# A batched x·yᵀ on one core: four half-stored rows remade in sixteen pieces, one for each DMA engine, and stored through GpSimd's queue

## The chip, the cores and the metric

The kernel runs on one core of a Trainium2 chip. The metric is device time in microseconds (us), lower is better. Before the change three runs took 297.93, 297.98 and 298.37 us, with a median of 297.98.

## The reference

```python
batch, n_heads, seq_t, seq_s, channels = 8, 12, 512, 512, 64
x: (8, 12, 512, 64) float32      y: (8, 12, 512, 64) float32
out = einsum('bhtc,bhsc->bhts', x, y)      # (8, 12, 512, 512) float32
```

For each of 96 (batch, head) pairs a 512 x 512 product of x with y transposed over 64 channels. 25.17 MB are read and 100.66 MB are written.

## The kernel before, in words

**Tiles.** The 96 heads are taken in 6 groups of 16, each group in two halves of 8 heads. A half makes 4 output tiles, so there are 48, numbered o = 0 to 47. A tile has 128 partitions of 4096 float32 (16 KB each, 2 MB in all) and covers two heads: partition p = 2q + u holds 8 full output rows (8 x 512) of head u, block q. Even partitions belong to one head, odd partitions to the other, and each partition is one contiguous 16 KB run in DRAM.

**Stages.** Loads of x and y (2 MB each, `load`, L177, on SyncE's queue, SP) are cast to bf16 and rearranged by ScalarE (ACT), VectorE (DVE) and GpSimd (POOL) in `compress` and `mix`, then transposed in 32 x 32 blocks by DVE (`transposes`, L225 and L234). TensorE (PE) makes a tile in two groups of four 128x512 matmuls (`products`, L248), one group into each of two PSUM buffers `pm0` and `pm1`. ACT copies PSUM into the output buffer (`copy`, L140); only the last tile, o = 47, is copied by DVE (L142). There are three pairs of output buffers (`pair`), each of two tiles.

**Stores.** All output goes through SP's hardware queue (queue 1 in the profile), but for a small share described below. Tiles 0 to 7 are stored one by one (2 MB). From tile 8 on, two tiles of one pair are stored together (4 MB, `transfer`, L161). The last four tiles are an exception: tile 44 (`SHARED`) is stored by `shares`, tile 45 alone (2 MB, L331), tiles 46 and 47 together (4 MB).

**What `shares` does.** Tile 44 is cut so that the core's 16 DMA engines get different amounts. The even partitions go in one transfer on SP's queue, 4 partitions to an engine. The odd partitions are taken in two halves b = 0 and b = 1. Of each half POOL's software queue (queue 0) takes three transfers, of 5, 3 and 8 engines with two partitions each: the first five engines get only columns 0 to 1023 of each partition (4096 B), the other eleven get the whole 16 KB. For the first four engines, SP's queue carries the remaining 3072 columns (`HELD` = 6 x 512; 12288 B). What is left are the 3072 **held columns** of the fifth engine's two partitions in each half: four rows of 12 KB, 48 KB, that this engine never carries.

**What `rest` does.** At the very end PE computes the held columns again (`again`, L298) into `pm0`: four pieces of 768 columns for each half, written in 20 small matmuls so that the pieces of one half lie in partitions 0 to 15. One DVE copy (L142, 16 x 1536) puts them into `xk0`, an input buffer that is no longer in use. Two SP transfers of 24 KB store them, each over four engines, two runs of 3072 B an engine and transfer. They are the last two transfers on SP's queue, behind the 4 MB store of tiles 46 and 47.

**Order and end.** The program order is written out by hand. `emit` waits for what an instruction needs, emits it and records it; `need` leaves out waits that are known to have been met. Each buffer's DMAs count on a semaphore of their own (`dma0`, `dma2`, ... for SP, `dmapool` for POOL). At the end POOL waits for all semaphores but two and clears them in three instructions (L412), then waits for `dmapool` and clears it, then for `dma2` (`LAST`, that of the 4 MB store and of the held pieces) and clears it (L415). That is the program's last instruction.

Of the kernel before, what the change touches and what calls it, by code (L numbers as in the profile page):

```python
# [9 lines left out]
def kernel(  # L10
# [3 lines left out]
    y: bass.AP,  # L14
    out: bass.AP,
):

# [4 lines left out]
    nc = tc.nc  # L24
    B, H, T, C = x.shape
    _, _, S, _ = y.shape
    P = 128
# [5 lines left out]
    V = G // 4  # L33
    K = 8
# [3 lines left out]
    N = K * S  # L38
    SINGLE = 2 * V
    SHARED = V * NH - V  # L40
    LAST = (V * NH - SINGLE - 2) // 2 % 3 * 2
    HELD = 6 * S
    fp32 = mybir.dt.float32
    bf16 = mybir.dt.bfloat16
    u32 = mybir.dt.uint32
# [9 lines left out]
    def buffer(name, width, dtype):  # L55
        return nc.alloc_sbuf_tensor(name, [P, width], dtype)[:, :]
# [4 lines left out]
    xks = [  # L61
        extra[:, :N // 2].bitcast(bf16) if i == 1 else buffer(f"xk{i}", R * C, bf16)
        for i in range(NG - 1)
    ]
# [9 lines left out]
    xTs = [buffer(f"xT{i}", K * D * E, u32) for i in range(2)]  # L74
    yTs = [buffer(f"yT{i}", D * R // 2, u32) for i in range(2)]
    pms = [nc.alloc_psum_tensor(f"pm{i}", [P, 4, S], fp32)[:, :, :] for i in range(2)]
    engines = {"act": nc.scalar, "dve": nc.vector, "pool": nc.gpsimd, "pe": nc.tensor, "sp": nc.sync}
    sems, ticks, snaps, writer, readers = {}, {}, {}, {}, {}
    known, own = {e: {} for e in engines}, {e: {} for e in engines}

    def need(name, points, told=True):

        best = {}
        for p, v in points:
            if known[name].get(p, 0) < v:
                best[p] = max(best.get(p, 0), v)
        for p, v in list(best.items()):
            if any(snaps[q, w].get(p, 0) >= v for q, w in best.items() if q != p):
                del best[p]
        for p, v in best.items():  # L90
            if told:
                engines[name].wait_ge(sems[p], v)  # L92
            known[name][p] = v
            for q, w in snaps[p, v].items():
                known[name][q] = max(known[name].get(q, 0), w)

    def promise(name, reads, writes):

        points = [writer[r] for r in (*reads, *writes) if r in writer]
        points += [v for w in writes for v in readers.get(w, ())]  # L100
        if name == "pool" and name in ticks:
            points.append((name, ticks[name]))
        return points

    def record(name, p, step, reads, writes, queue=False):
        at = (p, ticks.get(p, 0) + step)
        ticks[p] = at[1]
        if not queue:
            own[name][p] = at[1]
        snaps[at] = {**known[name], **own[name], p: at[1]}  # L110
        for r in reads:
            readers.setdefault(r, []).append(at)
        for w in writes:
            writer[w], readers[w] = at, []

    def signal(p):
        if p not in sems:
            sems[p] = nc.alloc_semaphore(p)
        return sems[p]

    def emit(name, make, reads=(), writes=(), dma=None, by=None, step=1):
        need(name, promise(name, reads, writes))
        p = by or name
        if dma is not None:
            p, step = f"dma{dma}", 16
        make().then_inc(signal(p), step)
        record(name, p, step, reads, writes, dma is not None)

    loaded = {}

    places = [0, 1, 2, 3, 4, 0, 1, 2, 3, 4, 1, 3]
    alone = [0, 2, 4, 0, 1, 3, 2, 4]
    heads = [0, 2, 1, 3]
# [3 lines left out]
    def copy(name, dst, src, reads, writes, by=None):  # L137
        emit(
            name,
            lambda: nc.scalar.activation(dst, src, COPY)  # L140
            if name == "act"
            else engines[name].tensor_copy(dst, src),  # L142
            reads,
            writes,
            by=by,
        )

    def both(*ids):
        return [("slot", i, pm) for i in ids for pm in range(2)]

    def place(ap, pattern):
        name = ap.tensor.name
        return mybir.PhysicalAccessPattern(
            ap=pattern, offset=ap.offset, dtype=ap.dtype, memref=name, memsetref=f"{name}_set"
        )

    def transfer(name, dst, src, to=None, of=None):

        to = to or dst.ap
        of = of or [src.ap[0], *[[1, 1]] * (len(to) - len(src.ap)), *src.ap[1:]]  # L160
        return engines[name].add_instruction(  # L161
            mybir.InstDMACopy(
                name=nc.get_next_instruction_name(),
                engine=engines[name].engine,
                ins=[place(src, of)],
                outs=[place(dst, to)],
                mode="Copy",
                cce_op=mybir.AluOpType.bypass,
                queue={"sp": "qSPDynamicHW", "pool": "qPoolDynamic"}[name],
            )  # L170
        )
# [82 lines left out]
    def all_products():  # L254
# [3 lines left out]
        with nc.Fori(1, V * NH + 1, 2 * V, engines=[nc.tensor.engine]) as first:  # L258
            for half in range(2):
                for j, h in enumerate(heads):  # L260
# [3 lines left out]
                    for p in range(2):  # L264
                        nc.tensor.wait_ge(sems[f"free{p}"], first + at)
                        products(half, h, 4 * p).then_inc(signal("pe"), 1)

    def shares(o, s):

        to, mine = ov[o // V, heads[o % V]], slots[s]  # L270
        line, w = to.ap[0][0], N - HELD

        def part(name, p, n, k, lo=0, hi=N):

            dst, src = to[p // 2:p // 2 + n, p % 2, lo:hi], mine[p:p + 2 * n - 1:2, lo:hi]
            emit(
                name, lambda: transfer(name, dst, src, [[line * n // k, k], [line, n // k], [1, hi - lo]]),
                reads=both(s), dma="pool" if name == "pool" else s,
            )

        for b in range(2):
            for p, n, k, hi in ((1, 10, 5, w), (21, 6, 3, N), (65, 16, 8, N)):
                part("pool", 32 * b + p, n, k, 0, hi)
        emit("sp", lambda: transfer("sp", to[:, 0], mine[::2]), reads=both(s), dma=s)
        for b in range(2):
            part("sp", 32 * b + 1, 8, 4, w)

    def again():

        half, h, part = SHARED // V % 2, heads[SHARED % V], HELD // 4  # L290
        xT = xTs[half].bitcast(bf16).rearrange("p (k h m) -> p k h m", k=K, h=V)
        yT = yTs[half].bitcast(bf16)
        for c in range(3, -1, -1):
            begin, end = N - HELD + c * part, N - HELD + (c + 1) * part
            cuts = sorted({begin, end, *range(begin, end, S), *(n for n in range(0, N, S) if begin < n < end)})
            for lo, hi in zip(cuts, cuts[1:]):
                for b in range(2):
                    last = nc.tensor.matmul(  # L298
                        pms[0][:4 * c + 4, 2 * b + (lo - begin) // S, (lo - begin) % S:(lo - begin) % S + hi - lo],
                        xT[:, lo // S, h, 32 * b + 16 - 4 * c:32 * b + 20],  # L300
                        yT[:, h * S + lo % S:h * S + lo % S + hi - lo], start=True, stop=True,
                    )
        return last

    def rest():

        half, part = SHARED // V % 2, HELD // 4
        to = ov[SHARED // V, heads[SHARED % V]]
        mine = xks[0][:16].bitcast(fp32)[:, :2 * part].rearrange("p (b s) -> p b s", b=2)
        emit("pe", again, [("xT", half), ("yT", half)], [("pm", 0)])  # L310
        copy(
            "dve", mine, pms[0][:16].rearrange("p (b j) s -> p b (j s)", b=2)[:, :, :part],
            [("pm", 0)], [("xk", 0)],
        )
        for b in range(2):
            dst, src = to[16 * b + 8:16 * b + 10, 1, N - HELD:], mine[1::2, b]
            emit(
                "sp", lambda: transfer(
                    "sp", dst, src, [[part, 4], dst.ap[0], [1, part]], [src.ap[0], [1, 1], src.ap[-1]]
                ),  # L320
                reads=[("xk", 0)], dma=LAST,
            )

    def store(o):
# [72 lines left out]
    for o in range(V, V * NH):  # L397
        result(o)
        if o % V == V - 1:
            prepare(o // V + 2)  # L400
    all_products()
    rest()
    emit("sp", nc.sync.nop)

    last = f"dma{LAST}"
    late = ["dmapool", last]
    others = [p for p in sems if p not in late]
    need("pool", [(p, ticks[p]) for p in others])
    numbers = sorted(sems[p].num for p in others)
    runs = [n for n in numbers if n - 1 not in numbers]  # L410
    for n in runs:
        nc.gpsimd.sem_clear(range(n, next(m for m in range(n, n + len(sems) + 1) if m not in numbers)))  # L412
    for p in late:
        need("pool", [(p, ticks[p])])
        nc.gpsimd.sem_clear(sems[p])  # L415


# [28 lines left out]
```

## Time and profile before

| | us |
|---|---|
| median of three runs | 297.98 |
| the profiled execution's own time | 297.92 |
| its span in the profile | 296.1 |
| outside the span | 1.8 |
| ACT busy | 208.2 |
| DVE busy | 158.0 |
| PE busy | 139.9 |
| POOL busy | 59.5 |
| written to and read from HBM | 125.8 MB, 425 GB/s over the span |

How to read it: the span runs from the first to the last instruction of the program. "Busy" leaves out waiting and the issuing of DMAs. The profile's page has a row of 40 digits for the DMA engines, the mean busy share of all 16 in tenths (9 is 90% or more), and the same row can be asked for over any stretch of time. A DMA is carried by several engines, each working through its own packets; the trace holds every packet with its queue, start, duration and size, though not with its engine. A transfer's packets end on each engine with one of 4 bytes, which counts up the semaphore.

### The profile page before, as it was taken

Reading aid. Unit: us, or ns where it says so; the run is one execution under the profiler, and the core shown is the slowest. Engines: PE = TensorE matmul, PEld = TensorE weight load, DVE = VectorE, ACT = ScalarE, POOL = GpSimd, SP = SyncE. Lnnn points to the kernel's source line nnn. Section 1 sums busy time; section 2 is a strip of 40 time slices with the busy share of each in tenths; the row PEclk is TensorE's granted clock in tenths of the full one; section 3 lists DMA queues with packets and bytes.
Section 4 is the critical chain, followed back from the end, with each engine's and each line's share of the span. In section 5 each row is a group of like instructions: output and inputs, shape, how many; then the busy total and the mean of one; then the engine's idle time right before and its main releaser. Section 6 shows DMA issues by size and latency. Waiting matters only on the chain.

```text
span 296.1 us, 1231 instructions
## 1 busy us (share of the span) xinstructions
PE 139.9 (47%) x404; PEld 37.9 (13%) x404; DVE 158.0 (53%) x76; ACT 208.2 (70%) x107; POOL 59.5 (20%) x29
## 2 busy tenths in 40 slices
PE   0000040437576557556654655577546646575400
PEld 0000010112111111111111111111111111121200
DVE  2167798899929594925808529258095240002600
ACT  1664666999999999666966696669666976684000
POOL 2399999992000000000000000000000000040000
PEclk9999995657779997778789776765798787756855
DMA  7999999999999999999999999999999999999998
GB/s 272 427 429 427 432 429 427 432 425 425 427 438 427 460 425 426 425 429 447 429 456 426 425 429 425 425 438 434 434 456 425 425 429 429 425 438 422 415 436 348
DMA packets 6178, 125.85 MB, mean 425 GB/s; under 512 B 896, under 2 KB 896, under 8 KB 932
## 3 DMA queue, kind: packets, MB, share of 16 engines
q1 hardware_dynamic: 5888, 125.03, 98.7%
q0 software_dynamic: 288, 0.80, 0.7%
q14 instruction: 2, 0.02, 0.0%
HBM read 25.17 MB, written 100.66 MB: 425 GB/s over the span
## 4 chain that ended last, share of the span: by engine, by line
DMA 56%; ACT 23%; PE 7%; issue 4%; DVE 3%; SPq 0%; ACTq 0%
DMA out_dram<-pair 43%; ACT pair L140 21%; DMA pair<-in_y_dram 7%; DMA pair<-in_x_dram 6%; PE pm L248 6%; DVE pair L142 3%; ACT xk L140 1%; PE pm L298 1%; ACT yb L140 1%; DVE xk L142 1%; SPq L177 0%; ACTq L92 0%; SPq L371 0%; SPq L367 0%
## 5 line engine op out<-in xcount | busy, mean ns | idle before, releaser
L248 PE MATMUL pm<-yT,xT 128*128 128x512 bf16 x384 | 136.6, 501 | 137.3 <-ACT pair L140 100.0
L140 ACT ACTIVATE pair<-pm 128x2048 f32<-128x2048 f32 x94 | 170.6, 1883 | 41.3 <-DMA out_dram<-pair 37.5
L225 DVE STREAM_TRANSPOSE xT<-xb 128x2048 uint32<-128x2048 uint32 x12 | 46.7, 3893 | 69.1 <-PE pm L248 66.7
L248 PEld LDWEIGHTS pm<-yT,xT 128*128 128x128 bf16 x384 | 36.0, 115 | 237.0 <-ACT pair L140 156.0
L161 POOL DMA_DIRECT2D out_dram<-pair x6 | 3.5, 583 | 193.7 <-ACT pair L140 193.7
L142 DVE COPY xb<-xk 32x2048 bf16<-32x2048 bf16 x32 | 41.7, 1304 | 0.9
L142 DVE CAST yb<-pair 64x2048 bf16<-64x2048 f32 x10 | 30.7, 3074 | 9.5 <-DMA pair<-in_y_dram 9.3
L140 ACT ACTIVATE xk<-pair 128x4096 bf16<-128x4096 f32 x5 | 18.1, 3617 | 10.4 <-DMA pair<-in_x_dram 10.3
L142 POOL COPY xb<-xk 32x2048 bf16<-32x2048 bf16 x8 | 23.5, 2939 | 6.7 <-ACT xk L140 6.2
L142 DVE COPY pair<-pm 128x2048 f32<-128x2048 f32 x2 | 4.5, 2286 | 31.9 <-PE pm L248 31.9
L234 DVE STREAM_TRANSPOSE yT<-yb 128x1024 uint32<-128x1024 uint32 x10 | 19.2, 1918 | 0.0
L140 ACT ACTIVATE yb<-pair 64x2048 bf16<-64x2048 f32 x5 | 12.4, 2472 | 3.9 <-DMA pair<-in_y_dram 3.8
L142 POOL CAST yb<-pair 64x2048 bf16<-64x2048 f32 x5 | 14.5, 2903 | 1.2 <-DMA pair<-in_y_dram 0.8
L142 POOL COPY xb<-pair 32x2048 bf16<-32x2048 bf16 x4 | 12.7, 3184 | 0.3
L140 ACT ACTIVATE pair<-pair 128x4096 bf16<-128x4096 f32 (+1 forms) x2 | 6.1, 3030 | 3.7 <-DMA pair<-in_x_dram 2.5
L142 DVE CAST pair<-pair 64x2048 bf16<-64x2048 f32 x2 | 5.4, 2694 | 4.0 <-DMA pair<-in_y_dram 4.0
L142 DVE COPY xb<-pair 32x2048 bf16<-32x2048 bf16 x4 | 5.2, 1306 | 0.1
L140 ACT ACT_TABLE_LOAD x1 | 1.3, 1283 | 4.4 <-PEq L371 4.4
L378 DVE MEMSET xb<- 128x2048 uint32 x1 | 1.8, 1765 | 4.9 <-PEq L371 4.9
L234 DVE STREAM_TRANSPOSE yT<-pair 128x1024 uint32<-128x1024 uint32 x2 | 3.9, 1946 | 0.0
L298 PE MATMUL pm<-yT,xT 128*16 128x256 bf16 (+5 forms) x20 | 3.3, 333 | 0.6 <-DVE pair L142 0.6
L142 POOL CAST pair<-pair 64x2048 bf16<-64x2048 f32 x1 | 3.3, 3293 | 0.1
(7 smaller groups left out, 5.8 us busy)
## 6 DMA issues: line engine op xcount, KB each, us to landing
out_dram<-pair SPq DMA_DIRECT2D x19, 4096.0 KB, 21.8
out_dram<-pair SPq DMA_DIRECT2D x9, 2048.0 KB, 9.3
pair<-in_x_dram SPq DMA_DIRECT2D x6, 2048.0 KB, 18.8
pair<-in_y_dram SPq DMA_DIRECT2D x6, 2048.0 KB, 16.5
out_dram<-pair SPq DMA_DIRECT2D x1, 1024.0 KB
out_dram<-pair POOLq DMA_DIRECT2D x2, 256.0 KB, 16.6
out_dram<-pair SPq DMA_DIRECT2D x2, 96.0 KB
out_dram<-pair POOLq DMA_DIRECT2D x2, 96.0 KB, 14.6
```

The source lines that it names most:

```text
L140: lambda: nc.scalar.activation(dst, src, COPY)
L142: else engines[name].tensor_copy(dst, src),
L161: return engines[name].add_instruction(mybir.InstDMACopy(name=nc.get_next_instruction_name(), engine=engines[name].engine, ins=[place(src, ...
L225: lambda: nc.vector.transpose(xTs[half].rearrange("p (k r e) -> p k e r", k=K, e=E), xbs[half].rearrange("p (k e c) -> p k e c", k=K, e=E),),
L234: lambda: nc.vector.transpose(yTs[half].rearrange("p (r j) -> p j r", r=D), ybs[half][b].rearrange("p (j c) -> p j c", c=D),),
L248: last = nc.tensor.matmul(pms[k // 4][:, j, :], xT[:, k + j, h, :], yT[:, h * S:(h + 1) * S], start=True, stop=True,)
L298: last = nc.tensor.matmul(pms[0][:4 * c + 4, 2 * b + (lo - begin) // S, (lo - begin) % S:(lo - begin) % S + hi - lo], xT[:, lo // S, h, 32 ...
L378: lambda: engines[name].memset(xbs[half], 0.0),
```

## The change

The held columns become 7 x 512 = 3584 for each of the four rows, 14 KB a row and 56 KB in all. So in `shares` the first five engines get 512 columns (2048 B) instead of 1024 of each partition through POOL's queue, and SP's two transfers for the first four engines grow to 14336 B a partition.

`again` now cuts the 3584 columns of each half into 8 pieces of 448 and makes them in 28 matmuls, so that piece q = 0 to 7 of half b lies in partitions 64b + 4q to 64b + 4q + 3, its two held rows in the second and fourth of them: partitions 0 to 31 and 64 to 95 in all. DVE's copy becomes 96 x 448. Instead of two SP transfers behind the 4 MB store, `rest` issues three transfers on POOL's queue, for 5, 3 and 8 engines, two runs of 448 columns (1792 B) an engine. At the end both late semaphores are waited for together and cleared in one instruction; the others too are cleared in one.

```diff
-    HELD = 6 * S
+    HELD = 7 * S
...
+    turns = [(0, 5), (5, 3), (8, 8)]
...
+    late = [f"dma{LAST}", "dmapool"]
+    for p in late:
+        signal(p)
...
+    def part(name, dst, src, k, reads, dma):
+        assert src.ap[0][1] == 2 * k and dst.ap[0][1] == k
+        emit(
+            name, lambda: transfer(name, dst, src, dst.ap),
+            reads=reads, dma=dma,
+        )
     def shares(o, s):
         to, mine = ov[o // V, heads[o % V]], slots[s]
-        line, w = to.ap[0][0], N - HELD
-        def part(name, p, n, k, lo=0, hi=N):
-            dst, src = to[p // 2:p // 2 + n, p % 2, lo:hi], mine[p:p + 2 * n - 1:2, lo:hi]
-            emit(
-                name, lambda: transfer(name, dst, src, [[line * n // k, k], [line, n // k], [1, hi - lo]]),
-                reads=both(s), dma="pool" if name == "pool" else s,
-            )
+        w = N - HELD
+        def odd(name, b, e, k, lo, hi):
+            p = 4 * e + 32 * b + (32 if e > 7 else 0)
+            n = 2 * k
+            dst = to[p // 2:p // 2 + n, 1, lo:hi].rearrange("(k i) n -> k i n", i=2)
+            part(name, dst, mine[p + 1:p + 2 * n:2, lo:hi], k, both(s), "pool" if name == "pool" else s)
         for b in range(2):
-            for p, n, k, hi in ((1, 10, 5, w), (21, 6, 3, N), (65, 16, 8, N)):
-                part("pool", 32 * b + p, n, k, 0, hi)
+            for e, k in turns:
+                odd("pool", b, e, k, 0, N if e else w)
         emit("sp", lambda: transfer("sp", to[:, 0], mine[::2]), reads=both(s), dma=s)
         for b in range(2):
-            part("sp", 32 * b + 1, 8, 4, w)
+            odd("sp", b, 0, 4, w, N)
     def again():
-        half, h, part = SHARED // V % 2, heads[SHARED % V], HELD // 4
-        xT = xTs[half].bitcast(bf16).rearrange("p (k h m) -> p k h m", k=K, h=V)
+        half, h, width = SHARED // V % 2, heads[SHARED % V], HELD // 8
+        xT = xTs[half].bitcast(bf16)
         yT = yTs[half].bitcast(bf16)
-        for c in range(3, -1, -1):
-            begin, end = N - HELD + c * part, N - HELD + (c + 1) * part
-            cuts = sorted({begin, end, *range(begin, end, S), *(n for n in range(0, N, S) if begin < n < end)})
-            for lo, hi in zip(cuts, cuts[1:]):
-                for b in range(2):
+        for b in (1, 0):
+            for q in range(7, -1, -1):
+                begin, end = N - HELD + q * width, N - HELD + (q + 1) * width
+                cuts = [begin, *(n for n in range(0, N, S) if begin < n < end), end]
+                for lo, hi in zip(cuts, cuts[1:]):
+                    stop = (lo // S * V + h) * P + 32 * b + 20
                     last = nc.tensor.matmul(
-                        pms[0][:4 * c + 4, 2 * b + (lo - begin) // S, (lo - begin) % S:(lo - begin) % S + hi - lo],
-                        xT[:, lo // S, h, 32 * b + 16 - 4 * c:32 * b + 20],
+                        pms[0][:64 * b + 4 * q + 4, 0, lo - begin:hi - begin],
+                        xT[:, stop - 64 * b - 4 * q - 4:stop],
                         yT[:, h * S + lo % S:h * S + lo % S + hi - lo], start=True, stop=True,
                     )
         return last
     def rest():
-        half, part = SHARED // V % 2, HELD // 4
+        half, width = SHARED // V % 2, HELD // 8
         to = ov[SHARED // V, heads[SHARED % V]]
-        mine = xks[0][:16].bitcast(fp32)[:, :2 * part].rearrange("p (b s) -> p b s", b=2)
+        mine = xks[0][:64 + 32].bitcast(fp32)[:, :width]
         emit("pe", again, [("xT", half), ("yT", half)], [("pm", 0)])
-        copy(
-            "dve", mine, pms[0][:16].rearrange("p (b j) s -> p b (j s)", b=2)[:, :, :part],
-            [("pm", 0)], [("xk", 0)],
-        )
-        for b in range(2):
-            dst, src = to[16 * b + 8:16 * b + 10, 1, N - HELD:], mine[1::2, b]
-            emit(
-                "sp", lambda: transfer(
-                    "sp", dst, src, [[part, 4], dst.ap[0], [1, part]], [src.ap[0], [1, 1], src.ap[-1]]
-                ),
-                reads=[("xk", 0)], dma=LAST,
+        copy("dve", mine, pms[0][:64 + 32, 0, :width], [("pm", 0)], [("xk", 0)])
+        for e, k in turns:
+            b, q = divmod(e, 8)
+            dst = to[16 * b + 8:16 * b + 10, 1, N - HELD + q * width:N - HELD + (q + k) * width]
+            p = 64 * b + 4 * q
+            part(
+                "pool", dst.rearrange("i (k n) -> k i n", n=width), mine[p + 1:p + 4 * k:2],
+                k, [("xk", 0)], "pool",
             )
...
-    last = f"dma{LAST}"
-    late = ["dmapool", last]
-    others = [p for p in sems if p not in late]
-    need("pool", [(p, ticks[p]) for p in others])
-    numbers = sorted(sems[p].num for p in others)
-    runs = [n for n in numbers if n - 1 not in numbers]
-    for n in runs:
-        nc.gpsimd.sem_clear(range(n, next(m for m in range(n, n + len(sems) + 1) if m not in numbers)))
-    for p in late:
-        need("pool", [(p, ticks[p])])
-        nc.gpsimd.sem_clear(sems[p])
+    for points in ([p for p in sems if p not in late], late):
+        need("pool", [(p, ticks[p]) for p in points])
+        numbers = [sems[p].num for p in points]
+        assert max(numbers) - min(numbers) == len(points) - 1
+        nc.gpsimd.sem_clear(range(min(numbers), max(numbers) + 1))
```

## The prediction, as put on record before the result

> **What bounds the kernel.** I read the page first: DMA digits, queues, chain.
>
> ```profile
> DMA  7999999999999999999999999999999999999998
> ...
> q1 hardware_dynamic: 5888, 125.03, 98.7%
> q0 software_dynamic: 288, 0.80, 0.7%
> ...
> DMA 56%; ACT 23%; PE 7%; issue 4%; DVE 3%; SPq 0%; ACTq 0%
> ```
>
> The 16 DMA engines are busy from the first slice to the last; the two queues' packets fill 99.4% of their time. So the kernel is bound by DMA time, and an edit at its end is worth only what it takes from the engine that finishes last. The timeline of the last stage shows when everything else is done:
>
> ```profile
> 262.35 3.48 POOL L161 DMA_DIRECT2D out_dram<-pair  x6 [193.71 <-ACT pair L140]
> ...
> 274.56 3.33 PE L298 MATMUL pm<-yT,xT 128*16 128x256 bf16 x20 [0.62 <-DVE pair L142]
> 276.73 0.58 SPq L161 DMA_DIRECT2D out_dram<-pair  x1
> 277.93 1.75 DVE L142 COPY xk<-pm 16x1536 f32<-16x1536 f32 x1 [1.23 <-PE pm L298]
> 279.70 2.00 SPq L161 DMA_DIRECT2D out_dram<-xk  x2
> ```
>
> Computing ends at 279.68, SP's issuing at 281.70; then the engines drain what is queued for 14 us more. The DMA view of 293.35 to 296.1 shows how they end (slices of 0.07 us; only packets that start in it are counted):
>
> ```profile
> DMA  9099999999990000000000002131313110000000
> ...
> DMA packets 56, 0.57 MB, mean 209 GB/s; under 512 B 24, under 2 KB 24, under 8 KB 40
> ```
>
> 56 packets are 16 last ones of 32 KB (one an engine), 16 of 3072 B (the held pieces) and 24 of 4 B (semaphore counts, 16 + 4 + 4). The low digits late in the row are the held pieces, on four engines only.
>
> From the trace's packet records I made one chain for each engine (a packet starts where the last of its engine ended). Each chain's own last packet ends at: the four engines with SP's pieces 295.49, 295.55, 295.66, **295.68**; the fifth 295.30; the other eleven 294.63 to **295.34**. The four end their 32 KB packets at 295.01 to 295.20 and spend the last 0.48 us on four held runs. The last count lands at 296.02, 0.34 us after its packet, and the last clear starts at 296.05.
>
> **The change part by part.** The price of bytes on one engine, from packet durations: 3072 B took 121 ns and 12288 B 463 ns, so 0.0371 ns per byte over 7 ns a packet; 1792 B comes to 73 ns (estimate from these rows).
>
> 1. *The four engines.* POOL's queue 4 x 4096 to 4 x 2048 B, SP's 4 x 12288 to 4 x 14336 B: these cancel. Held 4 x 3072 = 12288 B becomes 2 x 1792 = 3584 B: -8704 B, -0.32 us. 295.68 becomes 295.36.
> 2. *The fifth engine.* 4 x 4096 becomes 4 x 2048 + 3584 B: -4608 B, -0.17 us: 295.13.
> 3. *The eleven others* get 2 x 1792 B that they did not have: +0.15 us, 295.34 becomes 295.49. They are now the last.
> 4. *Counts.* The trace has 288 packets on queue 0 for six transfers: 64 of data (20 of 4096 B, 44 of 16 KB) and 224 of 4 B. That is what six transfers give if an engine with data has one packet of 4 B and one without has three (32 x 1 + 64 x 3). So three new transfers put 2 of data and 7 of 4 B on each engine. A 4 B packet takes 9 ns: +0.06 us for every engine, 295.55.
> 5. *POOL's descriptor work.* In 265 to 267.3, as the six transfers of before were being issued, 32 KB packets took 1253 ns on average (longest 1384), against 1215 from 150 to 262: 0.08 us an engine. For three transfers 0 to 0.08; I take 0.04, half of six: 295.59.
> 6. *Last waits.* Before, the wait for `dma2` sits in the last clear, which starts 0.03 us after the landing. Now one clear has two waits. Its nearest row is the earlier wait for two semaphores: landing 286.07, wait over at 286.10, clear at 286.14, 0.07 after the landing. +0.04 us; bounds 0 and 0.1.
>
> The end moves from 295.68 to 295.59, -0.09, plus 0.04: **-0.05 us**. Of 297.92 in the profiled execution (span 296.1 and 1.8 around it) that leaves 297.87; of the median, 297.98, 297.93. I take 297.90. Bounds of the unknown steps: 0 for 4, 5 and 6 gives -0.19, twice their sum +0.09; and the eleven engines' last end, which scatters over 0.7 us here, can fall 0.2 either way: 297.55 to 298.2.
>
> **What is hidden.** PE makes 7168 columns instead of 6144. At the row's spacings (0.214 us for 256 columns in the first 1.03 us, 0.108 after) that is 3.7 us instead of 3.35, and if a matmul under 256 columns can't be spaced closer than a weight load of the row takes (0.1 us), 4.3: PE ends at 278.3 to 278.9. DVE's copy is 448 columns long instead of 1536. From 2286 ns for 2048 and 1745 for 1536, 1.06 ns a column: 0.6 us instead of 1.75, done at 278.9 to 279.5. POOL then issues three transfers (the six before took 3.48 us; one 0.56 to 0.70): 279.0 to 281.3. POOL has nothing else; behind its waiting transfers stand only the clears, whose first wait was met at 286.07. SP loses two issues, which nothing waited for. Three fewer clears on POOL (44 to 88 ns each) ended by 286.5 and cost nothing. All this lies beside the engines' draining.
>
> The cover: a packet of queue 0 must reach its engine before queue 1 runs dry at about 295. Two DMA views bound this, 262.3 to 267.6 and 267.6 to 283.74:
>
> ```profile
> q1 hardware_dynamic: 80, 2.13, 94.9%
> ```
>
> ```profile
> q1 hardware_dynamic: 316, 6.05, 88.0%
> q0 software_dynamic: 288, 0.80, 12.5%
> ```
>
> From the first issue at 262.35 no queue 0 packet runs for 5.3 us; then all 288 run, and in the chains one packet of queue 0 stands after each packet of queue 1. The new ones, issued from 279.2, come at 284.5 by that row. Each engine has nine, one after each packet of queue 1, which are 32 KB and 1.22 us long from 285.5 on: the ninth comes at 284.5 + 9 x 1.22 = 295.5, just about where queue 1 ends. So the cover is used up, but its end costs little: a packet takes its engine's time wherever it stands, and those that are left when queue 1 is dry follow back to back. It is lost only if the first comes after 295.2, 16 us after its issue.
>
> **Rivals.**
>
> *A. The ends even out.* All 16 chains end at 295.13 on average, and the change moves bytes without adding any (4 x -8704 - 4608 + 11 x 3584 = 0). If the eleven engines' scatter is not fixed but follows load, the end comes near that mean, 295.23 with steps 4 and 5, and 0.04 for step 6: -0.41 us, **297.5**. For it: 15 engines then carry 69120 B each of tile 44's odd rows. Against: the eleven carry equal bytes already and still scatter by 0.7 us.
>
> *B. Slower: POOL's transfers land last.* The page's issue table:
>
> ```profile
> out_dram<-pair POOLq DMA_DIRECT2D x2, 256.0 KB, 16.6
> ...
> out_dram<-pair POOLq DMA_DIRECT2D x2, 96.0 KB, 14.6
> ```
>
> If 16.6 us is a delay of the queue itself, the third transfer, issued at about 280.5, lands at 297.1 instead of 296.02: +1.1 us, **299.0**. It decides from 15.5 us of issue to landing on. Against it: queue 0's 18 packets an engine ran in 16 us (267.6 to 283.7) one for one with queue 1's; once that is dry, nothing holds the new ones back.
>
> *C. POOL's descriptors slow a few engines.* The slowing of step 5 sums to 16 x 0.08 = 1.3 us over all engines. If three transfers cost as much and it falls on two of the eleven, that is 0.64 us each: 295.55 + 0.64 = 296.19, +0.5 us, **298.4**. Here it was spread over many packets (32 of 32 KB, 40 ns more on average, none over 171). The Trainium skill, "DMA: Bandwidth & Descriptors", Latency and other measured facts, says that engines 7 and 15 are usually slower, with contention at the descriptor rings of GpSimd's queue as its best guess; by that rule, which speaks against this change, case C is the way it goes. The trace does not agree so far: the chain that lags, landing 1.3 to 1.9 us after the other fifteen at several 4 MB stores before (237.32 and 238.72, 266.40 and 268.27), is the fifth engine's, and it lags before queue 0 is used at all.
>
> *D. The change doesn't do what it says*: the three transfers do not fall on 16 different engines. Then some engine has 3584 B more and another none: +0.15 us at most, inside the forecast's range.
>
> **How the numbers follow.** About 0.2% (0.6 us) is what a measurement of this kernel can tell from no change. Forecast (D within it) 0.72, A 0.12, B 0.05, C 0.06, something unnamed 0.05. Faster than 297.38: a third of A (0.04) and 0.02 of the unnamed, 0.06. Slower than 298.58: B, 0.01 of C and 0.03 of the unnamed, 0.09. Range 297.45 to 298.4, A's and C's times.
>
> **What would show it.** The tail of 3072 B packets is gone, and the last 32 KB packets end between 295.0 and 295.6. Queue 0 has 432 packets (288 + 32 of data + 112). DVE's copy of 96x448 takes 0.6 us, and POOL's three issues end by 281.5. The forecast is wrong if queue 0's first new packet comes after 295 (B), if 32 KB packets after 281 take over 1.3 us on few engines (C), or if the 16 last ends lie within 0.3 us (A).

## The result, and the profile after

The changed kernel takes **298.96 us** (median of 9 runs, 298.80 to 299.18) against 298.00 us for the kernel before in the same rounds (297.88 to 298.40). The ratio is 1.0031, with a 95% interval of 1.0022 to 1.0040: slower by 0.3%, where 297.9 and no change were forecast, and above the forecast's range of 297.45 to 298.4. The profiled execution took 298.80 us; its span grew from 296.1 to 297.0 us, and 1.8 us lie outside it as before. So the loss is inside the span.

The page of the changed kernel, DMA digits, queues and chain:

```profile
DMA  7999999999999999999999999999999999999996
...
q1 hardware_dynamic: 5864, 125.01, 98.4%
q0 software_dynamic: 352, 0.82, 0.7%
q8 instruction: 1, 0.02, 0.0%
q14 instruction: 2, 0.02, 0.0%
...
DMA 61%; ACT 24%; PE 4%; issue 4%; DVE 2%; SPq 0%; ACTq 0%
```

Two things differ from before. The last digit has fallen from 8 to 6: most engines are done while the span goes on. And there is a queue that was not there, **queue 8, "instruction", one packet** of 16 KB. (Queue 14 with its two packets stands on the page of before too.) It shows as 0.0% of 16 engines' time and is easy to pass over.

The timeline of the last stage went as the change says:

```profile
273.77 5.39 PE L313 MATMUL pm<-yT,xT 128*96 128x448 bf16 x28
...
276.33 0.58 SPq L168 DMA_DIRECT2D out_dram<-pair  x1
...
279.20 0.62 DVE L149 COPY xk<-pm 96x448 f32<-96x448 f32 x1 [2.89 <-PE pm L313]
280.12 1.70 POOL L168 DMA_DIRECT2D out_dram<-xk  x3 [14.22 <-DVE xk L149]
```

Queue 0's new packets start at 284.75 and are through by 292.77. But the DMA view from 293.35 to 297 (slices of 0.09 us, packets counted by their start) ends differently:

```profile
DMA  0099098988008000000008000000000000000000
...
DMA packets 33, 0.56 MB, mean 153 GB/s; under 512 B 16, under 2 KB 16, under 8 KB 16
```

The tail of held pieces is gone, as forecast: there are only 32 KB packets and 16 counts. Of the 32 KB packets one starts alone, at 295.27, when ten engines have finished and the other five are within 0.44 us of their end. The 16 engines end their last 32 KB packets at 294.83 to 295.41, 295.71 and **296.48** (295.68 was the end of all packets before). One engine is 0.77 us behind the next.

That engine is the one that carried queue 8's packet: followed packet by packet, each starting within some ns of the end of the one before, the row from 276.33 to the last packet at 295.27 has it. The DMA view of 276 to 281, and that engine's packets in the trace (start, duration, size):

```profile
q1 hardware_dynamic: 141, 1.70, 82.1%
q0 software_dynamic: 124, 0.32, 16.4%
q8 instruction: 1, 0.02, 1.2%
```

```
276.79   918 ns   16384 B  queue 1        (others of this size: 611 ns)
277.72   898 ns   16384 B  queue 1
278.62   931 ns   16384 B  queue 8
279.54   999 ns   16384 B  queue 1
```

The packet takes 0.93 us and the three next to it 0.31, 0.29 and 0.39 us more than the usual 0.611: **1.91 us of one engine's time**. Without them it would have ended at 294.57 (an estimate: 296.48 - 1.91), among the first. It has 16 KB packets on queue 0 in tile 44's odd rows, so it is one of the eleven.

### The profile page after: what moved, and what is told of

It is laid out like the page before. It is cut to its first block, busy times and chain, and to the rows that moved or that the text cites. A ratio compares the mean times of both kernels' runs of the same rounds, so it can differ in the third digit from the quotient of the medians.

```text
span 297.0 us, 1246 instructions
## 1 busy us (share of the span) xinstructions
PE 141.6 (48%) x412; PEld 39.2 (13%) x412; DVE 157.1 (53%) x76; ACT 208.4 (70%) x107; POOL 61.3 (21%) x32
## 4 chain that ended last, share of the span: by engine, by line
DMA 61%; ACT 24%; PE 4%; issue 4%; DVE 2%; SPq 0%; ACTq 0%
DMA out_dram<-pair 47%; ACT pair L147 22%; DMA pair<-in_y_dram 7%; DMA pair<-in_x_dram 6%; PE pm L255 4%; DVE pair L149 2%; ACT xk L147 1%; ACT yb L147 1%; SPq L184 0%; ACTq L95 0%; SPq L383 0%; SPq L379 0%
## 5 line engine op out<-in xcount | busy, mean ns | idle before, releaser
L313 PE MATMUL pm<-yT,xT 128*96 128x448 bf16 (+27 forms) x28 | 5.4, 372 | 0.0
L168 POOL DMA_DIRECT2D out_dram<-xk x3 | 1.7, 569 | 14.2 <-DVE xk L149 14.2
```

The source lines that it names most:

```text
L168: return engines[name].add_instruction(mybir.InstDMACopy(name=nc.get_next_instruction_name(), engine=engines[name].engine, ins=[place(src, ...
L313: last = nc.tensor.matmul(pms[0][:64 * b + 4 * q + 4, 0, lo - begin:hi - begin], xT[:, stop - 64 * b - 4 * q - 4:stop], yT[:, h * S + lo % ...
```

## The experiments

Theory P: the packet is a block of TensorE's instructions, fetched because the eight further closing matmuls made its program longer. Theory Q: it is fetched for GpSimd, which issues three transfers more. Theory R: the packet matters little, and GpSimd's transfers make the loss. Each run was timed beside the kernel before.

**Only the matmuls.** The kernel before, with two cuts made over again, 28 matmuls instead of 20:

```diff
-        for c in range(3, -1, -1):
+        for c in (3, 2, 2, 2, 1, 0):
```

> The kernel before, with eight of its 20 closing matmuls (two cuts of four) made again, so that there are 28; nothing else differs and the output is the same. Theory P (the 16 KB packet of queue 8 in the profile after is a block of TensorE's instructions, fetched because TensorE's program became eight matmuls and eight weight loads longer; it holds up one DMA engine by 1.9 us): the packet appears here too, one engine ends later, and the time is 0.4 to 1.2 us above the kernel before (298.4 to 299.2). Theory Q (the packet is fetched for GpSimd, which issues three more transfers): no such packet, no change (within 0.2 us). Theory R (the packet matters little, GpSimd's small packets make the loss): no change.

298.76 us against 298.05, ratio 1.0025 (1.0016 to 1.0034). The page of this kernel:

```profile
q0 software_dynamic: 288, 0.80, 0.7%
q8 instruction: 1, 0.02, 0.0%
```

GpSimd's queue is untouched at 288 packets, and the packet on queue 8 is there: 938 ns, its three neighbours 944, 860 and 999 ns. One engine ends its last 32 KB packet at 296.33, the next at 295.46. P holds, Q and R fall: eight matmuls at an idle TensorE, with nothing else changed, make most of the loss.

**All but the matmuls.** The changed kernel without its first eight closing matmuls:

```diff
+        made = 0
...
+                    made += 1
+                    if made <= 8:
+                        continue
                     stop = (lo // S * V + h) * P + 32 * b + 20
```

> The changed kernel with the first eight of its 28 closing matmuls left out, so that there are 20 as before; the columns that they made keep what PSUM held. All else is as in the changed kernel, its three transfers on GpSimd's queue too. Theory P: no packet on queue 8, 297.8 to 298.1, the forecast's 297.9. Theory Q: the packet stays, 298.9 to 299.0. Theory R: no change against the changed kernel, 298.9 to 299.0, whether or not the packet is there.

297.81 us, ratio to before 0.9994 (0.9985 to 1.0003). No queue 8 on its page, and the DMA view from 293.35 to 297 ends in one block:

```profile
DMA  0009899998000000000000000000000000000000
...
DMA packets 32, 0.52 MB, mean 144 GB/s; under 512 B 16, under 2 KB 16, under 8 KB 16
```

All 16 last 32 KB packets start within 0.6 us; they end at 294.86 to 295.42. This is the change as the forecast thought of it, and it comes out within 0.1 us of the forecast. Against the kernel before in the same rounds (298.05) it is 0.24 us less by the medians, where 0.05 less was forecast; the interval of the ratio reaches 1.0003, so a gain is not shown.

**Without GpSimd's transfers.** The changed kernel with its three closing transfers on SP's queue:

```diff
             part(
-                "pool", dst.rearrange("i (k n) -> k i n", n=width), mine[p + 1:p + 4 * k:2],
-                k, [("xk", 0)], "pool",
+                "sp", dst.rearrange("i (k n) -> k i n", n=width), mine[p + 1:p + 4 * k:2],
+                k, [("xk", 0)], LAST,
             )
```

> The changed kernel with its three closing transfers on SP's queue behind the 4 MB store instead of GpSimd's, still 28 matmuls. They fall on the first 5, 3 and 8 engines, so three engines get three pieces and some get none. Theory P: the packet on queue 8 stays and one engine ends late: 298.7 to 299.1. Theory Q: no packet, since GpSimd issues as many transfers as before: 297.9 to 298.2. Theory R: 297.9 to 298.2.

298.85 us, ratio 1.0028 (1.0017 to 1.0039). Its page has less on queue 0 than before, and queue 8 all the same:

```profile
q1 hardware_dynamic: 5912, 125.07, 98.5%
q0 software_dynamic: 256, 0.76, 0.6%
q8 instruction: 1, 0.02, 0.0%
```

The packet stands at 278.73 with 929 ns, and one engine ends at 296.43, 1.1 us behind the next. Q and R fall again.

**How many matmuls.** The changed kernel without its first six, four and two closing matmuls (22, 24 and 26 left; same edit as above).

> The changed kernel with the first six of its 28 closing matmuls left out (22 stay; the columns that they made keep what PSUM held). Theory P: 20 and 22 lie on the near side of a block's end or 22 on the far side; so either 297.7 to 298.0 with no packet and 1.8 us between span and time, or 298.7 to 299.1 with a packet after the span or 2.1 to 2.9 us there. Nothing between. Rival P2 (each matmul costs): 298.0 to 298.2, a quarter of the loss.

> The changed kernel with the first four of its 28 closing matmuls left out (24 stay; the columns that they made keep what PSUM held). Theory P: somewhere between 20 and 28 the packet appears, and with it a step, not a slope: either no packet and about 297.8, or the packet and 298.6 to 299.0. Rival P2: a slope, about half of the loss, 298.3 to 298.5.

> The changed kernel with the first two of its 28 closing matmuls left out (26 stay; the columns that they made keep what PSUM held). As with 24: by theory P either no packet and about 297.8 or the packet and 298.6 to 299.0; by rival P2 three quarters of the loss, 298.5 to 298.7.

| closing matmuls | median us | ratio to before (interval) | span / outside it, profiled execution | executions with neither / a long span / a long time outside |
|---|---|---|---|---|
| 20 | 297.81 | 0.9994 (0.9985 to 1.0003) | 295.8 / 1.8 | 11 / 0 / 0 |
| 22 | 297.86 | 1.0001 (0.9991 to 1.0011) | 295.9 / 1.8 | 9 / 0 / 1 |
| 24 | 299.00 | 1.0033 (1.0021 to 1.0045) | 296.0 / 2.8 | 0 / 3 / 3 |
| 26 | 298.92 | 1.0025 (1.0015 to 1.0035) | 295.9 / 2.1 | 2 / 5 / 1 |
| 28 | 298.96 | 1.0031 (1.0022 to 1.0040) | 297.0 / 1.8 | 0 / 9 / 0 |

The last column sorts the executions of each kernel: a long span is 296.8 us or more, a long time outside is 2.7 us or more. The kernel before has neither in any of the 80 executions for which both are on record (span at most 296.6, outside at most 2.2).

It is not a slope: P2, by which each matmul costs its share, falls. Most of the step lies between 22 and 24, but it is not sharp, since one of the ten executions with 22 took 299.25, with 3.1 us outside the span. The profiled execution with 24 does not have the longer span; its loss lies behind the span. The DMA view of it from 296.5 to 299.5, after its last instruction at 296.0:

```profile
DMA  0000000000000000009000000000000000000000
...
DMA packets 1, 0.02 MB, mean 5 GB/s; under 512 B 0, under 2 KB 0, under 8 KB 0
...
q8 instruction: 1, 0.02, 2.4%
```

The same packet, alone, at 297.91 for 1171 ns, when the kernel's own work is done. So the loss has two forms. Either the packet comes early enough to hold up an engine that is still draining, and the span is long, or it comes after the last instruction, and the time outside the span is long; either way about 1 us. With 28 matmuls all nine executions have the first form, and with 24 and 26 both forms occur in one and the same kernel. Only profiled executions show the packet itself; for the others this is inferred from span and time. How the late packet lengthens the program's closing is not shown: it ends at 299.08, later than that execution's own time of 298.84 us can reach if this begins no later than the span. With 26 the eight runs fall into two groups (297.87 and 297.99; six of 298.86 to 299.11), and the profiled execution, 297.99, is of the first and shows no packet.

**The same length without matmuls.** The kernel before, and ahead of TensorE's loop 16 bare counts of a spare semaphore:

```diff
+    for _ in range(16):
+        emit("pe", nc.tensor.nop, by="spare")
     all_products()
```

> The kernel before with 16 bare counts of a spare semaphore on TensorE ahead of its loop (nothing waits for them until the end), as many instructions as eight matmuls with their weight loads. Theory P (a block of TensorE's instructions): the length alone counts, so the 16 KB packet on queue 8 appears near the end as in the changed kernel and the time is 298.7 to 299.0. Rival P2 (the closing matmuls themselves, their number or their later end, call the packet): no packet, 297.9 to 298.2.

298.75 us, ratio 1.0026 (1.0017 to 1.0035), as expected of P: the matmuls' time has no part in it. But the packet does not stand on the page: the profiled execution is one of the two shortest (298.34; runs from 297.90 to 299.46). Of the eleven executions four have the long span (296.9 to 297.0) and five the long time outside (2.75 to 3.36), so both forms occur here too, as with 24 and 26 matmuls and not as with 28. What decides between them was not found out.

**The block fetched early.** The changed kernel with 184 such counts ahead of the loop:

```diff
+    for _ in range(184):
+        emit("pe", nc.tensor.nop, by="spare")
     all_products()
```

> The changed kernel, all 28 closing matmuls, with 184 bare counts of a spare semaphore on TensorE ahead of its loop, so that the block's end lies before the loop and the block is fetched while TensorE still waits for the first inputs. Theory P: the packet on queue 8 moves to the first 60 us, where the engines meet again at each load and store (the last of 16 lands within 0.02 us of the others up to 90 us), and the time is that without the packet, 297.7 to 298.1. If only the packet's presence counts and not its place, 298.7 to 299.0. Rival P2: 298.7 to 299.0.

298.50 us, ratio 1.0010 (1.0001 to 1.0019). The packet did move, into the DMA view of 58 to 62:

```profile
q1 hardware_dynamic: 112, 1.61, 95.1%
q8 instruction: 1, 0.02, 1.7%
```

(at 58.76, 1068 ns). But the time came only half way back, and my reason for 297.7 to 298.1 was wrong. From the landings of each store, how far the last of 16 engines is behind the fifteenth:

```
last of 16 lands at    57.76  63.80  73.53  92.89  141.37  189.81
behind the fifteenth    0.20   1.15   1.13   1.15    0.60    0.06
```

The lag arises at the packet and stays at 1.15 us for 30 us. It shrinks afterwards only because another engine, one that falls behind steadily in every run here, comes up from the other side; from about 200 us on that one is last. So here, where the engines always have work queued, a lag stays. That the last engine lands 0.02 us behind the fifteenth up to 87 us in the kernel before does not mean that something brings the engines together: the first of the 16 lands 0.5 to 0.8 us ahead of the fifteenth all that time. At the end the engine that carried the block still lands 0.73 us behind (296.64, the next 295.92). Two of the eleven executions (297.88 and 298.03) are as short as those without a block; where the packet stood in them is not known.

**Fewer matmuls by the cut.** The changed kernel with seven pieces of 512 columns (none crosses a row of 512, so 14 matmuls), and with six pieces and 6 x 512 held columns (12 matmuls; `range(5, -1, -1)` and transfers of 4, 2 and 6 engines). The edit for seven:

```diff
-        half, h, width = SHARED // V % 2, heads[SHARED % V], HELD // 8
+        half, h, width = SHARED // V % 2, heads[SHARED % V], S
...
-            for q in range(7, -1, -1):
+            for q in range(6, -1, -1):
...
-        half, width = SHARED // V % 2, HELD // 8
+        half, width = SHARED // V % 2, S
...
-        for e, k in turns:
+        for e, k in ((0, 5), (5, 2), (8, 7)):
```

> The changed kernel with the 3584 held columns of each half cut into seven pieces of 512 instead of eight of 448, so that no piece crosses from one 512-column row to the next and 14 matmuls do it; three GpSimd transfers of 5, 2 and 7 engines, two runs of 2048 B an engine, two engines without. Theory P: no packet on queue 8, 297.7 to 298.0. Theories Q and R: as the changed kernel, 298.9 to 299.0.

> The changed kernel with 6 x 512 held columns as before and six pieces of 512 for each half: 12 closing matmuls, three GpSimd transfers of 4, 2 and 6 engines. Theory P: no packet; against seven pieces the fifth engine carries 8192 B more (0.30 us) and two more engines get none, so 297.7 to 298.0 and no gain over seven pieces. If fewer matmuls are in themselves faster (P2): below seven pieces' 297.8 by 0.05 to 0.1.

Seven pieces: 297.81 us, ratio to before 0.9991 (0.9982 to 1.0000), no queue 8, and a DMA view from 293.35 to 297 that again ends in one block, three slices longer than with 20 matmuls:

```profile
DMA  0009899988888000000000000000000000000000
```

Six pieces: 297.92 us, 0.9996 (0.9987 to 1.0005), no queue 8. Between 12 and 22 matmuls there is no order by number. Seven pieces, the same output as the changed kernel with the same 56 KB held, is 1.15 us below it and, at the edge of its interval, no slower than the kernel before.

## Why the prediction was wrong

The step that failed is the first part of **"What is hidden"**: "PE makes 7168 columns instead of 6144 ... All this lies beside the engines' draining." The time of the eight matmuls does lie beside it (TensorE ended at 279.16, DVE's copy at 279.82). What I did not count is that they are also 16 more instructions, and that TensorE's program comes to it through the same DMA engines that bound the kernel. The Trainium skill, "Runtime: NRT & Kernel Launch", Instruction fetch mechanics, says that each engine's instructions are refilled in blocks of 16 KiB by DMA and calls the cost of crossing a block's end mostly hidden. The size agrees with the packet of 16384 B; that it is hidden does not: 1.91 us of one engine, 0.9 us of the span.

Step by step, with the kernel of 20 matmuls as the change without the block:

- *The end.* 295.59 was forecast for the last engine; it was 295.42 with 20 matmuls and 295.68 with seven pieces. Steps 1 to 3 hold: the four engines' tail is gone, and the ends stand within 0.6 to 0.8 us of each other.
- *Step 4* was too large: queue 0 has 352 packets, not 432. The two runs of 1792 B went as one packet of 3584 B and 140 ns, not two of 73, and each engine got six new packets, not nine.
- *Step 5*, 0.04 us: 32 KB packets that started after 281 took 1224 ns instead of 1219, eight an engine: 0.04 us.
- *Step 6*: the last clear started 0.02 us after the landing, not 0.07. Nothing was added.
- *The sizes in "What is hidden"*: PE took 5.39 us, not 3.7 to 4.3 (the granted clock was 0.50 from 273.7 to 276.0 and 0.68 from there to 279.2), DVE's copy ended at 279.82, not by 279.5, and POOL's issues at 281.82, not 281.3. All three still ended 13 us before the engines did.
- *The cover*: the first new packet at 284.75 (284.5 forecast), the last done at 292.77, 2 us ahead of queue 1's end.

*Rivals.* A did not come (0.6 us of scatter remains). B fell: POOL's packets end at 292.77; that its 299.0 is close to the time measured is chance. C has the right shape, one engine held up late, but its cause is refuted: on SP's queue the loss is the same, and with POOL's transfers but 20 matmuls it is gone. D fell with steps 1 to 3. The loss belongs to the "something unnamed" for which 0.03 was kept on the slower side.

What is not settled: where in TensorE's program the block's end lies to the instruction, and why, with 22 to 26 matmuls or 16 counts, one and the same kernel shows the loss now inside the span, now behind it and now not at all. That the packet is TensorE's rests on two kernels in which only TensorE's program was changed and in which it came (28 matmuls in the kernel before) or moved (184 counts).

## What to carry to other kernels

Where the DMA engines bound a kernel, count an edit's instructions and not only their time: an engine with nothing to do still draws its program through them, in blocks, and here two small matmuls more (24 for 22) took the loss from one execution in ten to all six. Look at the page's queue rows for an "instruction" packet that was not there, and at the span and at what lies outside it separately. And an engine that has fallen behind in such a kernel stays behind, so a block fetched at 59 us is still felt at the end (298.50 us here, against 297.81 with no block and 298.96 with one at 279 us).

## What the hardware showed beyond that

- A 16 KB instruction packet took 929 to 938 ns beside stores near the end, 1068 ns at 58.76 and 1171 ns with no other packet beside it; a 16 KB store packet takes 611.
- Only its own engine pays: in the changed kernel no packet of another engine that started between 276 and 281 took more than 0.06 us over the usual time of its size, while the three next to the block took 0.29 to 0.39 us more each.
- In the kernel before, one engine falls behind the fifteenth by itself: 0.03 us at the landing of 91.68, 0.51 at 130.97, 0.98 at 199.54, 1.87 at 268.27. The cause stays open.
